# Moving a weight read behind a head's operands, cutting GpSimd's operations into 256-column pieces, and computing three kinds of small factors on ScalarE

## The chip, the cores and the metric

One core of a Trainium2 chip runs the whole program. The metric is the device time in microseconds (us) of one execution. The engines are TensorE (PE), which multiplies, VectorE (DVE), ScalarE (ACT) and GpSimd (POOL), which do the elementwise work, and SyncE (SP), which here issues the DMA transfers.

## The reference

The kernel computes a two-layer decoder trunk for 512 tokens of width 1024 in float32. Between two feed-forward halves each layer has a mixer of three groups of heads that run side by side on one input projection:

```python
for l in range(DEPTH):                                  # DEPTH = 2
    x = x + 0.5 * swiglu(rmsnorm(x, ffn1_norm[l]), ffn1_wg[l], ffn1_wu[l], ffn1_wd[l])
    h = rmsnorm(x, mix_norm[l]) @ w_in[l]
    h_a, h_b, h_c = jnp.split(h, [A_COLS, A_COLS + B_COLS], axis=-1)
    o_a = mla_mixer(h_a, ...)       # 6 heads, low-rank q and kv, rope on 32 of 96 columns
    o_b = nsa_mixer(h_b, ...)       # 6 heads: compressed, selected and window attention, gated
    o_c = diff_mixer(h_c, ...)      # 4 heads: softmax 1 - lam * softmax 2
    x = x + jnp.concatenate([o_a, o_b, o_c], axis=-1) @ w_out[l]
    x = x + 0.5 * swiglu(rmsnorm(x, ffn2_norm[l]), ffn2_wg[l], ffn2_wu[l], ffn2_wd[l])
return rmsnorm(x, final_norm)

# nsa_mixer: g = sigmoid(gate_logits); o = g0 * o_cmp + g1 * o_slc + g2 * o_win
#            compress: silu(blocks @ w1) @ w2
# diff_mixer: o = o1 - lam * o2, then a norm over each head's 64 columns
```

## The kernel before

Activations lie transposed in SBUF: 128 features on the partitions, 512 tokens in the free dimension. To keep float32 accuracy each operand of a matmul is split into a rounded high part and the rest (`split`: ACT copies or scales into `hi`, and DVE or POOL subtracts it for `lo`, L162 and L164, or L166 with a scale), and each product takes three passes (`mm3`, `mm3y`: hi*hi, hi*lo, lo*hi).

A layer goes ffn1, mix, ffn2. The feed-forward parts stream weights through `weights()`: a 512 KB read into `raw`, then a split into `whl`. While ffn1 runs, `split_ahead` does this for the eight column groups of `w_in` named in `AHEAD = (2, 0, 1, 3, 9, 8, 5, 4)` and parks the split pair of 1 MB in a DRAM buffer (`pre<-whl`). In the mix `weights()` finds the key in `PRE` and needs a read only (`whl<-pre`, L185).

The mix first projects the columns of the C heads (differential attention). Each result is split and written to two DRAM buffers by `put` (`part<-b`, L755), and `c_load(h)` reads one head's operands back in another layout: six reads `qk<-part` (L194) for head 0, then six for each further head. The period table `PLAN` then sets the order of PE's work in the rest of the mix: in each row the front (scores) of one head, the back (weighing the values) of the head before it, and `items` such as `p2 p0 cl1 cl2` (projections of column groups 2 and 0, loads of C heads 1 and 2) are interleaved step by step. A front (`scores`) computes score rows in PSUM; DVE takes the negated row maximum (`nmx`, L595), ACT the exponential with the row sum (`pn`, L596), DVE a reciprocal; `turned` transposes the probabilities on PE (`pst`, L573), and ACT and DVE split them into `pt`. In `c_front` the second softmax's factor is multiplied by -lam (L825), ACT scales the rows of the second softmax with it (L827), and DVE adds the rows of the first (L828). At L886 to L890 the NSA gate is made: exp on ACT, plus one on DVE (L889), reciprocal on DVE. L1020 to L1022 do the same for the silu of the compression.

PE's order within the mix is the program's. The order of the other engines and of SP's queue is set when the kernel is built, by a scheduler with a timeline of its own. POOL takes `split`s with `eng=gp` (the weight tiles 128x1024 and others, the query heads in `SPARE`), the products of the rotary embedding (`rope`, `roped`, `a_query`: L556, L557, L729, L730, L952, L953), the slow reciprocal root (`rsqrt_slow`: L211, L212, L214) and one sum of squares (L866).

## Time and profile before

| quantity | value |
|---|---|
| median of 3 runs | 2020.51 us (2019.13 to 2026.75) |
| the profiled execution | 2023.87 us |
| its span in the trace | 2022.1 us |
| PE busy | 1968.2 us (97%) |
| DVE busy | 1473.4 us (73%) |
| ACT busy | 1066.5 us (53%) |
| POOL busy | 253.5 us (13%) |
| DMA queue of SP | 286.48 MB, 45.5% of 16 engines' span |

Times inside the profile count from the start of the span. Busy shares are means over stages with different limits: in the two feed-forward parts PE has no gaps, and most of its idle time lies in the two mixes (about 380 to 660 us and 1380 to 1660 us) and at the two ends of the program. The profiled execution lies 3.36 us above the median of the three runs, and inside their range.

### The profile page before, as it was taken

To read this page: it belongs to the slowest core of one execution; us is meant where nothing else is said; L and a number is where in the kernel's file an instruction comes from. 1 tells how busy PE (TensorE), PEld (TensorE's weight loads), DVE (VectorE), ACT (ScalarE), POOL (GpSimd) and SP (SyncE) were. 2 spreads that over 40 slices of the span, in tenths; PEclk is the share of its full clock that TensorE was granted. 3 is DMA by queue.
4 is the path that set the end of the run, shared out by engine and by line. 5 is a ranking of instruction groups with operands and counts; after the bars stand their busy time and mean duration, and the time that the engine had idled before them with its cause. 6 is when DMAs were issued, how large, how long until landed. Compare 5 with 4: busy or idle time off the path is not lost.

```text
span 2022.1 us, 31129 instructions
## 1 busy us (share of the span) xinstructions
PE 1968.2 (97%) x11864; PEld 1711.7 (85%) x11864; DVE 1473.4 (73%) x2315; ACT 1066.5 (53%) x2010; POOL 253.5 (13%) x183
## 2 busy tenths in 40 slices
PE   8999999989999999999999999999989999999997
PEld 6899988867777899998889999887668778999886
DVE  8888874478887888883378887444898878888623
ACT  4455643266687545562255556333667764555521
POOL 5000001025420100001100000110354010000011
PEclk9999999999999999999999999999999999999999
DMA  6333388664632523334442335777447143333431
GB/s 209 105 105 105 114 282 266 207 213 129 179 105 81 170 94 105 105 118 138 131 143 88 106 107 170 245 230 228 158 135 214 53 146 115 95 106 106 133 114 55
DMA packets 104549, 288.46 MB, mean 143 GB/s; under 512 B 14928, under 2 KB 18768, under 8 KB 104400
## 3 DMA queue, kind: packets, MB, share of 16 engines
q1 hardware_dynamic: 104400, 286.48, 45.5%
q8 instruction: 93, 1.52, 0.3%
q14 instruction: 56, 0.46, 0.1%
HBM read 237.77 MB, written 46.66 MB: 141 GB/s over the span
## 4 chain that ended last, share of the span: by engine, by line
PE 83%; DVE 8%; DMA 2%; ACT 2%; issue 2%; SPq 1%; POOL 1%; DVEq 0%; ACTq 0%; POOLq 0%
PE psm L562 19%; PE psm L203 14%; PE pss L562 11%; PE pst L203 10%; PE pst L562 9%; PE pss L203 8%; PE pso L562 6%; PE pso L203 5%; PE pst L573 1%; DVE nmx L595 1%; DVE pt L164 1%; DMA part<-b 1%; DVE b L166 1%; DMA qk<-part 1%; SPq L194 1%
## 5 line engine op out<-in xcount | busy, mean ns | idle before, releaser
L162 ACT CAST whl<-raw 128x1024 fp32r<-128x1024 f32 (+2 forms) x417 | 383.8, 923 | 489.8 <-issue 104.8
L164 DVE TENSOR_TENSOR whl<-raw,whl 128x1024 fp32r<-128x1024 f32 (+2 forms) x383 | 420.1, 1099 | 222.2 <-ACT whl L162 221.4
L562 PE MATMUL psm<-b,whl 128*128 128x256 f32 (+1 forms) x2140 | 448.6, 346 | 3.6 <-DVE t L951 3.6
L562 PEld LDWEIGHTS psm<-b,whl 128*128 128x128 f32 x2140 | 328.8, 192 | 44.5 <-issue 8.0
L203 PE MATMUL psm<-b,whl 128*128 128x512 f32 (+1 forms) x948 | 230.6, 383 | 1.2 <-DVE whl L164 1.0
L298 POOL TENSOR_TENSOR t<-t,t 128x512 f32<-128x512 f32 x48 | 78.3, 1632 | 1104.2 <-ACT t L292 777.4
L203 PEld LDWEIGHTS psm<-b,whl 128*128 128x128 f32 x948 | 174.7, 189 | 36.5 <-DVE whl L164 1.4
L203 PE MATMUL pst<-b,whl 128*128 128x512 f32 x624 | 158.6, 394 | 3.0 <-DVE b L166 1.2
L203 PEld LDWEIGHTS pst<-b,whl 128*128 128x128 f32 x624 | 117.3, 189 | 31.3 <-DVE b L166 3.1
L596 ACT ACTIVATE pn<-pss,nmx 128x256 f32<-128x256 f32 x208 | 109.6, 528 | 64.6 <-DVE nmx L595 63.3
L595 DVE TENSOR_REDUCE nmx<-pss 128x1 f32<-128x256 f32 x208 | 97.7, 485 | 42.2 <-PE pss L562 30.9
L203 PE MATMUL pss<-b,whl 128*128 128x512 f32 x504 | 126.3, 390 | 0.0
L562 PE MATMUL psm<-qk,whl 128*128 128x256 f32 x840 | 123.7, 284 | 0.0
L562 PE MATMUL pst<-b,whl 128*128 128x256 f32 (+1 forms) x816 | 121.2, 290 | 0.2 <-DVE b L164 0.2
L562 PE MATMUL pss<-b,whl 128*128 128x256 f32 (+1 forms) x816 | 120.8, 290 | 0.0
L562 PEld LDWEIGHTS psm<-qk,whl 128*128 128x128 f32 x840 | 111.2, 192 | 0.3
L203 PEld LDWEIGHTS pss<-b,whl 128*128 128x128 f32 x504 | 94.7, 188 | 19.5
L562 PEld LDWEIGHTS pst<-b,whl 128*128 128x128 f32 x816 | 108.5, 192 | 2.9 <-DVE b L164 0.5
L562 PEld LDWEIGHTS pss<-b,whl 128*128 128x128 f32 x816 | 108.9, 192 | 2.1
L164 DVE TENSOR_TENSOR whl<-pn,whl 128x1024 fp32r<-128x1024 f32 x63 | 77.2, 1226 | 26.2 <-ACT whl L162 26.2
L562 PE MATMUL pst<-qk,whl 128*128 128x256 f32 x576 | 84.8, 284 | 0.0
L562 PE MATMUL pss<-qk,whl 128*128 128x256 f32 x576 | 84.8, 283 | 0.0
(314 smaller groups left out, 3402.6 us busy)
## 6 DMA issues: line engine op xcount, KB each, us to landing
raw<-in_ffn_gu_dram SPq DMA_DIRECT2D x174, 512.0 KB, 3.7
raw<-in_ffn_d_dram SPq DMA_DIRECT2D x64, 512.0 KB, 3.7
pre<-whl SPq DMA_DIRECT2D x16, 1024.0 KB, 5.5
whl<-pre SPq DMA_DIRECT2D x16, 1024.0 KB, 7.0
raw<-in_w_in_dram SPq DMA_DIRECT2D x28, 512.0 KB, 6.0
raw<-in_ffn_d_dram SPq DMA_DIRECT2D x32, 384.0 KB, 3.4
xin<-xs SPq DMA_DIRECT2D x48, 256.0 KB, 3.0
raw<-in_w_out_dram SPq DMA_DIRECT2D x32, 256.0 KB, 2.8
```

The lines of the kernel that those rows point to most:

```text
L162: high = sc.copy(hi, src) if scale is None else sc.mul(hi, src, scale)
L164: eng.tensor_tensor(lo, src, f32(hi), op=ALU.subtract)
L166: eng.scalar_tensor_tensor(lo, src, scale, f32(hi), op0=ALU.mult, op1=ALU.subtract)
L194: return sy.dma_start(f32(dst), f32(src))
L203: pe.matmul(ps, w(a), x(b), start=first and k == 0 and j == 0, stop=last and k == n - 1 and j == 2)
L298: gp.tensor_tensor(sq, sq, self.acc, op=ALU.add)
L562: return tc.keep_in_program_order(pe.matmul(*args, **kw))
L573: return tc.keep_in_program_order(pe.transpose(dst, src, idn))
L595: ve.reduce_max(nmx, part[i], axis=AX.X, negate=True)
L596: sc.activation(pn[i], part[i], AF.Exp, bias=nmx, accum_out=sm[:, i:i + 1])
```

## The change

It does three things. First, `c_load` keeps the last of head 0's six operand reads in `S["cl0"]`, and the read of a pre-split weight tile in `project` (`whl<-pre`) is put behind it in the order of issue, for every column group but the first of `AHEAD`. Secondly, a helper `pieces` issues a `tensor_tensor` of POOL with a 2-dimensional output as pieces of 256 columns; it is used by `split`, `rsqrt_slow`, `rope`, `roped`, `a_query` and the sum L866. Calls with DVE as the engine go through it unchanged, and POOL's other operations (L294, L296, L298, L326, L1078, L1079) don't use it. Thirdly, three kinds of small steps become ACT instructions: the factor times -lam, and the two "plus one" steps of the gate and of the silu, which add a constant tile `onet` as bias.

```diff
--- before.py
+++ after.py
@@ -157,11 +157,19 @@
     def f32(ap):
         return ap.bitcast(F32) if ap.dtype == F32R else ap
 
+    def pieces(eng, o, a, b, op):
+
+        n = o.shape[1]
+        m = P * 2 if eng is gp and len(o.shape) == 2 else n
+        for c in range(0, n, m):
+            d = min(c + m, n)
+            eng.tensor_tensor(o[:, c:d], a[:, c:d], b[:, c:d], op=op)
+
     def split(src, hi, lo, scale=None, eng=ve):
 
         high = sc.copy(hi, src) if scale is None else sc.mul(hi, src, scale)
         if scale is None:
-            eng.tensor_tensor(lo, src, f32(hi), op=ALU.subtract)
+            pieces(eng, lo, src, f32(hi), op=ALU.subtract)
         else:
             eng.scalar_tensor_tensor(lo, src, scale, f32(hi), op0=ALU.mult, op1=ALU.subtract)
         return high
@@ -178,11 +186,12 @@
         d = PRE[key] = dp.tile([P, 2, 8 * P], F32, name=nm("pre"))
         sy.dma_start(d, f32(hl[:, :, :8 * P]))
 
-    def weights(src, rows=P, cols=8 * P, eng=gp, key=None):
+    def weights(src, rows=P, cols=8 * P, eng=gp, key=None, behind=None):
 
         if key in PRE:
             hl = wp.tile([P, 2, WPAD], F32R, tag="whl", name=nm("whl"), bufs=WHLS)
-            sy.dma_start(f32(hl[:, :, :8 * P]), PRE.pop(key))
+            with tc.issue_after(behind.ins) if behind else ExitStack():
+                sy.dma_start(f32(hl[:, :, :8 * P]), PRE.pop(key))
             return hl
         raw, hl = weight_tiles()
         sy.dma_start(raw[:rows, :cols], src)
@@ -208,10 +217,10 @@
         sc.activation(y, ps, AF.Ln, bias=epst, scale=mul)
         sc.activation(ms, ps, AF.Identity, bias=epst, scale=mul)
         sc.activation(y, y, AF.Exp, scale=-0.5)
-        gp.tensor_tensor(r, y, y, op=ALU.mult)
-        gp.tensor_tensor(r, r, ms, op=ALU.mult)
+        pieces(gp, r, y, y, op=ALU.mult)
+        pieces(gp, r, r, ms, op=ALU.mult)
         sc.activation(r, r, AF.Identity, bias=halft, scale=-0.5)
-        gp.tensor_tensor(r, r, y, op=ALU.mult)
+        pieces(gp, r, r, y, op=ALU.mult)
         return r
 
     def rsqrt(ps, mul, r):
@@ -264,6 +273,8 @@
     gp.memset(epst, EPS)
     halft = cp.tile([P, 1], F32, name="halft")
     gp.memset(halft, 1.5)
+    onet = cp.tile([P, 1], F32, name="onet")
+    gp.memset(onet, 1.0)
 
 
     xs = [I["xT"]]
@@ -553,8 +564,8 @@
         t, sw = tmp()[r0:r1], tmp()[r0:r1]
         ve.stream_shuffle(sw, src, swap)
         ve.tensor_tensor(t, src, cos[r0:r1], op=ALU.mult)
-        eng.tensor_tensor(sw, sw, sin[r0:r1], op=ALU.mult)
-        eng.tensor_tensor(t, t, sw, op=ALU.add)
+        pieces(eng, sw, sw, sin[r0:r1], op=ALU.mult)
+        pieces(eng, t, t, sw, op=ALU.add)
         return t
 
     def mm(*args, **kw):
@@ -693,7 +704,8 @@
 
         def project(c, done, eng=gp):
 
-            w = weights(I["w_in"][l, c], eng=ve if "w%d" % c in SPARE else eng, key=("in", l, c))
+            w = weights(I["w_in"][l, c], eng=ve if "w%d" % c in SPARE else eng, key=("in", l, c),
+                        behind=S.get("cl0") if c != AHEAD[0] else None)
             pj = psum("m")
             yield from mm3y(pj, [((lambda a, k=k: w[:, a, k * P:(k + 1) * P]), (lambda b, k=k: xg[k][:, b])) for k in range(KD)])
             done(pj)
@@ -726,8 +738,8 @@
             c, sw = tmp()[:n], tmp()[:n]
             ve.stream_shuffle(sw, t[:n], swap)
             ve.tensor_tensor(c, t[:n], loaded(tabs[g, 0])[:n], op=ALU.mult)
-            eng.tensor_tensor(sw, sw, loaded(tabs[g, 1])[:n], op=ALU.mult)
-            eng.tensor_tensor(t[:n], c, sw, op=ALU.add)
+            pieces(eng, sw, sw, loaded(tabs[g, 1])[:n], op=ALU.mult)
+            pieces(eng, t[:n], c, sw, op=ALU.add)
             return t
 
         def scales(n):
@@ -811,7 +823,8 @@
                 src = S["C"][c].rearrange("j (d h m) n -> j d h (m n)", h=4, m=2)[:, :, h]
                 dst = qk[c].rearrange("p m n -> p (m n)")
                 for j in range(3):
-                    move(dst[32 * j:32 * j + 32], src[PASS[j][1 - c]])
+                    done = move(dst[32 * j:32 * j + 32], src[PASS[j][1 - c]])
+            S.setdefault("cl0", done)
 
         def c_front(h):
             qk = S["cqk", h]
@@ -822,7 +835,7 @@
                 ve.reciprocal(o[1], o[1])
                 pns.append(o)
             (p1, s1), (p2, s2) = pns
-            ve.tensor_scalar(s2, s2, S["nlam"], None, op0=ALU.mult)
+            sc.mul(s2, s2, S["nlam"])
             for j in range(NT):
                 sc.mul(p2[j], p2[j], s2[:, j:j + 1])
                 ve.scalar_tensor_tensor(p1[j], p1[j], s1[:, j:j + 1], p2[j], op0=ALU.mult, op1=ALU.add)
@@ -863,7 +876,7 @@
             t = S["at1"] = scaled(pj, rs[0])
             q = tmp()
             sc.activation(q[:64], t[:64], AF.Square)
-            gp.tensor_tensor(S["aq0"][:64], S["aq0"][:64], q[:64], op=ALU.add)
+            pieces(gp, S["aq0"][:64], S["aq0"][:64], q[:64], op=ALU.add)
             ca1 = S["ca1"] = halves(t[:64], mg[:64, 1:2])
 
             kp = rope(t[64:96], loaded(tabs[0, 0]), loaded(tabs[0, 1]), SWAP16, 64, 96)
@@ -886,7 +899,7 @@
             gate = S["gate"] = small([P, NT, 32], "gate", bufs=1)
             gf = gate.rearrange("p i c -> p (i c)")
             sc.activation(gf, gps[:, :P], AF.Exp, scale=-1.0)
-            ve.tensor_scalar(gf, gf, 1.0, None, op0=ALU.add)
+            sc.activation(gf, gf, AF.Identity, bias=onet)
             ve.reciprocal(gf, gf)
             yield
 
@@ -949,8 +962,8 @@
             t, sw = tmp(), tmp()
             ve.tensor_tensor(t[:96], pj[:96], ta[:96, 0], op=ALU.mult)
             ve.stream_shuffle(sw[64:96], pj[64:96], SWAP16)
-            gp.tensor_tensor(sw[64:96], sw[64:96], ta[64:96, 1], op=ALU.mult)
-            gp.tensor_tensor(t[64:96], t[64:96], sw[64:96], op=ALU.add)
+            pieces(gp, sw[64:96], sw[64:96], ta[64:96, 1], op=ALU.mult)
+            pieces(gp, t[64:96], t[64:96], sw[64:96], op=ALU.add)
             split(t[:96], q[:96, 0], q[:96, 1], eng=gp if "hq%d" % h in SPARE else ve)
 
         def a_front(h):
@@ -1018,7 +1031,7 @@
             ve.scalar_tensor_tensor(z[:, :, 0:31], p3[0:64, :, 0:31], bias, y1[:, :, 1:32], op0=ALU.add, op1=ALU.add)
             e = small([64, 2, 32], "ce", bufs=1)
             sc.activation(e, z, AF.Exp, scale=-1.0)
-            ve.tensor_scalar(e, e, 1.0, None, op0=ALU.add)
+            sc.activation(e, e, AF.Identity, bias=onet[:64])
             ve.reciprocal(e, e)
             ve.tensor_tensor(z, z, e, op=ALU.mult)
             zh = S["z", n] = small([64, 2, 64], "czh", F32R)
```

The number of PE's instructions and their order stay as they were. DVE has 14 instructions fewer, ACT 14 more, and POOL 117 more. All lines of the changed file lie further down (L185 becomes L194, L194 becomes L203, L755 becomes L767, L595 and L596 become L606 and L607, L162 and L164 become L170 and L166, which is `pieces`).

SP's queue at the start of layer 0's mix, ahead of the first C head; `whl` are weight tiles, `pre` the parked split weights, `part` the DRAM buffers of the C heads, `qk` the head operands. Before:

```order
L185 DMA whl_3845<-pre_2808 128x2x1024
L755 DMA part_3535<-b_3642 64x2x512
L755 DMA part_3536<-b_3642 64x2x512
L194 DMA qk_3647<-part_3535 32x1024 x3
L194 DMA qk_3648<-part_3536 32x1024 x3
L194 DMA qk_3914<-part_3535 32x1024 x3
L194 DMA qk_3915<-part_3536 32x1024 x3
L194 DMA qk_3922<-part_3535 32x1024 x3
L194 DMA qk_3923<-part_3536 32x1024 x3
L185 DMA whl_3957<-pre_2960 128x2x1024
L185 DMA whl_4043<-pre_3060 128x2x1024
```

And with the change:

```order
L767 DMA part_3537<-b_3644 64x2x512
L767 DMA part_3538<-b_3644 64x2x512
L203 DMA qk_3649<-part_3537 32x1024 x3
L203 DMA qk_3650<-part_3538 32x1024 x3
L194 DMA whl_3847<-pre_2810 128x2x1024
L203 DMA qk_3916<-part_3537 32x1024 x3
L203 DMA qk_3917<-part_3538 32x1024 x3
L203 DMA qk_3924<-part_3537 32x1024 x3
L203 DMA qk_3925<-part_3538 32x1024 x3
L194 DMA whl_3959<-pre_2962 128x2x1024
```

The weight read `whl_3845` (now `whl_3847`, column group 0) stood ahead of the last two writes of `part`; now it stands behind them and behind the first six `qk` reads, and twelve more `qk` reads follow it. Layer 1 moves in the same way.

DVE at the NSA gate in layer 0, between the row maxima of two heads; `gate` is the gate tile. Before:

```order
L728 TENSOR_TENSOR t_4101<-t_4099,xin_4104 128x512
L595 TENSOR_REDUCE nmx_4176<-pss_4172 128x1
L889 TENSOR_SCALAR gate_4153<-gate_4153 128x128
L890 RECIPROCAL gate_4153<-gate_4153 128x128
L595 TENSOR_REDUCE nmx_4179<-pss_4172 128x1
L595 TENSOR_REDUCE nmx_4185<-pss_4182 128x1
L595 TENSOR_REDUCE nmx_4205<-pss_4202 128x1
```

And with the change:

```order
L740 TENSOR_TENSOR t_4106<-t_4104,xin_4109 128x512
L606 TENSOR_REDUCE nmx_4186<-pss_4182 128x1
L903 RECIPROCAL gate_4163<-gate_4163 128x128
L606 TENSOR_REDUCE nmx_4189<-pss_4182 128x1
L606 TENSOR_REDUCE nmx_4195<-pss_4192 128x1
L606 TENSOR_REDUCE nmx_4215<-pss_4212 128x1
```

The sum L889 is gone from between the maximum and the reciprocal; ACT has it now as L902, ahead of the exponential of the same head.

DVE at the fourth C head in layer 0; `sm` are the head's factors, `pn` its probabilities, `t` and `b` the work of other heads. Before:

```order
L164 TENSOR_TENSOR peh_5063<-pe_5061,peh_5063 64x32
L822 RECIPROCAL sm_4407<-sm_4407 128x4
L720 TENSOR_TENSOR t_4512<-psm_4467,rstd_3499 128x512
L825 TENSOR_SCALAR sm_4407<-sm_4407,nlam_3545 128x4
L166 SCALAR_TENSOR_TENSOR b_4438<-t_4167,dn_3539,b_4438 128x512
L166 SCALAR_TENSOR_TENSOR b_4514<-t_4512,b_4514 128x512
L828 SCALAR_TENSOR_TENSOR pn_4331<-pn_4331,sm_4332,pn_4406 128x128
L828 SCALAR_TENSOR_TENSOR pn_4331<-pn_4331,sm_4332,pn_4406 128x256
L828 SCALAR_TENSOR_TENSOR pn_4331<-pn_4331,sm_4332,pn_4406 128x384
L828 SCALAR_TENSOR_TENSOR pn_4331<-pn_4331,sm_4332,pn_4406 128x512
L632 TENSOR_TENSOR t_4565<-pso_4524,t_4565 64x512
```

And with the change:

```order
L166 TENSOR_TENSOR peh_5104<-pe_5102,peh_5104 64x32
L835 RECIPROCAL sm_4420<-sm_4420 128x4
L732 TENSOR_TENSOR t_4531<-psm_4486,rstd_3501 128x512
L174 SCALAR_TENSOR_TENSOR b_4454<-t_4177,dn_3541,b_4454 128x512
L174 SCALAR_TENSOR_TENSOR b_4533<-t_4531,b_4533 128x512
L643 TENSOR_TENSOR t_4584<-pso_4543,t_4584 64x512
L841 SCALAR_TENSOR_TENSOR pn_4344<-pn_4344,sm_4345,pn_4419 128x128
L841 SCALAR_TENSOR_TENSOR pn_4344<-pn_4344,sm_4345,pn_4419 128x256
L841 SCALAR_TENSOR_TENSOR pn_4344<-pn_4344,sm_4345,pn_4419 128x384
L841 SCALAR_TENSOR_TENSOR pn_4344<-pn_4344,sm_4345,pn_4419 128x512
```

The factor L825 is gone from between the two products, and the sum L632 (now L643) stands ahead of the four row sums L828 (now L841) instead of behind them.

## Rows read from the trace of the kernel before

**Rows 1.** The page, busy time of each engine: PE.

```profile
PE 1968.2 (97%) x11864; PEld 1711.7 (85%) x11864; DVE 1473.4 (73%) x2315; ACT 1066.5 (53%) x2010; POOL 253.5 (13%) x183
```

**Rows 2.** PE's waits over the whole span: total us, times, longest.

```profile
PE pss L562 <- ACT pn L596: 9.8, 19, 1.8
...
PE pss L562 <- DMA qk<-part: 6.1, 2, 4.0
```

**Rows 3.** Timeline of PE: start, us, instructions; in brackets the wait before and its releaser.

```profile
401.54 0.42 PE L562 MATMUL pss<-qk,qk 96*128 96x256 f32 x2 [2.12 <-DMA qk<-part]
...
407.61 2.09 PE L562 MATMUL psm<-b,whl 128*128 128x512 f32 x8
...
439.27 0.50 PE L562 MATMUL pss<-qk,qk 96*128 96x512 f32 x1 [1.82 <-ACT pn L596]
...
482.40 0.41 PE L573 MATMUL pst<-cst,pn 128*128 128x128 f32 x2 [2.25 <-DVE pt L164]
...
1400.17 0.66 PE L562 MATMUL pss<-qk,qk 96*128 96x256 f32 x2 [3.97 <-DMA qk<-part]
```

**Rows 4.** Windows behind those waits: window us, PE busy, PEclk, DMA share, GB/s.

```profile
401.82:405.23 3.41, 3.41 (x12) 0.50 1.01 233
483.74:487.15 3.41, 3.41 (x15) 0.50 0.87 223
1398.52:1405.35 6.83, 5.18 (x15) 0.50 1.01 234
```

**Rows 5.** Timeline of SP's queue, 386 to 404: start, us to issue, transfers.

```profile
386.81 0.56 SPq L185 DMA_DIRECT2D whl<-pre  x1
387.46 2.15 SPq L755 DMA_DIRECT2D part<-b  x2
395.71 8.23 SPq L194 DMA_DIRECT2D qk<-part  x18
```

**Rows 6.** The chain that ended last, three of its pieces: start, us, what.

```profile
387.46 8.10 DMA part<-b
...
397.96 3.34 DMA qk<-part
...
1385.56 10.30 DMA part<-b
```

**Rows 7.** DMA to landing: first L755's six writes from 380.8, then all of L185.

```profile
DMA to landing us min/median/max: 4.9/5.9/6.1
...
DMA to landing us min/median/max: 5.2/7.0/10.8
```

**Rows 8.** Windows of 20 us: PE, PEld, DVE, ACT, POOL, PEclk, DMA share, GB/s.

```profile
400.00:420.00 20.00, 17.91 (x76) 13.16 (x77) 10.35 (x24) 11.61 (x32) 1.56 (x1) 0.91 1.01 286
...
500.00:520.00 20.00, 17.24 (x87) 12.61 (x88) 18.36 (x35) 11.04 (x27) 13.96 (x9) 0.95 0.48 139
```

**Rows 9.** DVE's groups by form, 395 to 560: busy us, mean ns, idle before.

```profile
L825 DVE TENSOR_SCALAR sm<-sm,nlam 128x4 f32<-128x4 f32 x4 | 2.5, 637 | 0.1
L889 DVE TENSOR_SCALAR gate<-gate 128x128 f32<-128x128 f32 x1 | 1.0, 985 | 0.0
```

**Rows 10.** Timelines of DVE and of POOL, 471 to 476.

```profile
472.10 1.87 DVE L825 TENSOR_SCALAR sm<-sm,nlam 128x4 f32<-128x4 f32 x1
473.88 1.85 DVE L166 SCALAR_TENSOR_TENSOR b<-t,dn,b 128x512 fp32r<-128x512 f32 x1
...
471.54 2.40 POOL L164 TENSOR_TENSOR whl<-raw,whl 128x1024 fp32r<-128x1024 f32 x1
473.89 1.29 POOL L164 TENSOR_TENSOR qk<-t,qk 96x512 fp32r<-96x512 f32 x1
```

**Rows 11.** POOL's groups by form, whole span: busy us, mean ns, idle before.

```profile
L164 POOL TENSOR_TENSOR whl<-raw,whl 128x1024 fp32r<-128x1024 f32 x10 | 24.8, 2478 | 6.7 <-ACT whl L162 6.2
...
L729 POOL TENSOR_TENSOR t<-t,xin 64x512 f32<-64x512 f32 x2 | 5.5, 2760 | 5.8 <-DVE t L727 5.8
L326 POOL TENSOR_TENSOR pn<-b,rstd 128x256 f32<-128x256 f32 x6 | 4.9, 849 | 15.1 <-DVE rstd L226 15.1
```

**Rows 12.** ACT's groups by form, 395 to 560: busy us, mean ns, idle before.

```profile
L888 ACT ACTIVATE gate<-pst 128x128 f32<-128x128 f32 x1 | 0.3, 278 | 0.0
```

## Prediction

> **What bounds the kernel now.** I read the busy line of the page first: TensorE (PE) works for 1968.2 of the 2022.1 us span [rows 1]. So nothing but PE's standstills and its slow stretches can be won, unless its matmuls change, and the change leaves all of them and their order alone. What is left is 53.9 us (2022.1 less 1968.2), and some of that is the start and the end of the program. Next I read PE's waits by releaser: 9.8 us for the exponentials of the score rows on ScalarE (ACT), and 6.1 us, in only two waits, for reads of `qk` tiles out of the DRAM buffer `part` [rows 2]. The timeline of PE then gives the places, and each of those this part speaks of recurs in layer 1, about 1000 us later: 2.12 and 3.97 us before the first C head's scores, 1.82 us at the NSA gate (1.81 in layer 1), and 2.25 us at the fourth C head (2.26 in layer 1) [rows 3]. [...]
>
> **Part 1: the read of the second pre-split weight tile goes behind the first head's operands.** The queue of SyncE (SP) issues six writes of `part`, then the 1 MB read `whl<-pre`, then the last two writes, and then the `qk` reads [rows 5]. The reads wait for the writes: the chain that ended last has 8.10 us in the writes behind the weight read, and then 3.34 us in the last `qk` read that the scores need [rows 6]. The first six writes, with no weight read straight ahead of them, landed 4.9 to 6.1 us after their issue [rows 7]. Without the read ahead, the pair starts at 386.81 in place of 387.46, and its last write, issued some 0.9 us later, lands by 387.7 + 4.9 to 6.1 = 392.6 to 393.8. SP's first `qk` issue in before was at 395.71 and the sixth read landed at 397.96 + 3.34 = 401.30, 5.6 us later; moved, that is 398.2 to 399.4. PE asks for it at 401.54 - 2.12 = 399.42: the wait goes. In layer 1 the writes took 10.30 us from 1385.56 [rows 6]; at 6.1 us, and 0.65 us earlier, they end at 1391.0 instead of 1395.9, 4.9 us sooner, and the 3.97 us wait goes as well. With the two half-clock stretches this removes 2.12 + 3.97 + 1.7 + 2.6 = 10.4 us.
>
> What is late next is the weight read itself. It now passes two writes and six `qk` issues and starts at 395 to 396 (sixth issue), while twelve more `qk` reads queue behind it, half a microsecond apart (8.23 us for 18 [rows 5]). Reads of this kind took 5.2 to 10.8 us, in the middle 7.0 [rows 7], and the DMA engines were full from 400 to 420 (share 1.01 [rows 8]). Issued at 395.8 it lands at 402.8, at worst at 406.6. Its first user is the matmul group at 407.61 [rows 3], which, with 2.12 + 1.7 us saved ahead of it, comes at 403.8. By the middle value the read is just hidden; by the worst PE waits 2.8 us, and some 1 us more in layer 1, where more time is saved ahead of the need. I charge 0.7 us per layer. **Part 1: 10.4 - 1.4 = 9.0 us gained**, at most 10.4, at least 3 (first rival).
>
> **Part 2: three kinds of small steps move from VectorE (DVE) to ACT.** For each layer these are four factors (128x4), one gate sum (128x128) and two 64x64 sums. On DVE they cost far more than their size: 637 ns mean for the 128x4, 985 for the 128x128 [rows 9]. The timeline shows why: the 128x4 step that began at 472.10 took 1.87 us and ended at 473.97, when GpSimd's (POOL) 1024-wide subtraction, begun at 471.54, ended at 473.94; the next DVE step, 1.85 us, ended after POOL's next one (473.89 to 475.18) [rows 10]. So a DVE instruction of this form stands behind the whole POOL instruction that is running. ACT does a 128x128 step in 278 ns [rows 12], and I take 0.25 us for each moved step, so 14 of them are 3.5 us on ACT over both layers, in places where it mostly waits for DVE. At the gate the DVE steps sum, reciprocal and the next row maximum stand in the way of the exponential that PE waits for. The sum's 0.98 us leaves that chain, since ACT has it ready while DVE still works on the maximum before it: 0.95 per layer, 1.9 in all. At the fourth C head 1.87 us leave DVE, ahead of the transposed rows that PE waits 2.25 us for: I take 1.8 per layer, 3.6 in all, and half of the one half-clock stretch there, 0.9. If ACT is full when its extra step comes, it costs up to its 0.25 us; this I expect at the first C head, 0.2 per layer.
>
> [...]
>
> **Part 3: POOL's 2-dimensional operations in the mix go in pieces of 256 columns**, 117 instructions more in both layers. A 1024-wide subtraction took 2478 ns, or 620 per 256 columns; the 256-wide operation that the kernel has took 849 [rows 11]. So a further piece costs at most 0.23 us, at least 0 if pieces overlap. I take 0.15 (nearer the upper end, since the 849 ns may hold waiting): 18 us of POOL time over two mixes, in which POOL has room. What it frees is DVE, which then waits for one piece of about 0.7 us and not for up to 2.48. Of PE's 9.8 us of waits for exponentials 1.82 + 1.81 were counted; of the 6.2 us left in 17 waits I take a third, 2.0 us, since here I can name no single piece that carries all. Against it 0.5 us for POOL results that come later. **Parts 2 and 3: 1.9 + 3.6 + 0.9 + 2.0 - 0.4 - 0.5 = 7.5 us gained**, between 0 (all of it turns into the next wait) and about 14 (most of the named waits and their clock).
>
> **Sum.** 9.0 + 7.5 = 16.5 us off. The profiled execution was 2023.87 us, 3.4 above the median of 2020.51, so it becomes 2007.4 and the median 2004.0.
>
> **The rivals.** (a) *The weight read takes the wait over.* For it: DMA is full there and 1 MB cannot land faster because it is put later. Against it: by the middle value it has 1 us to spare. At 10.8 us PE waits 2.8 us and 3.8 us in the two layers: with 1.4 already charged that takes 5.2 more, and a clock fall 1.4: 2010.6. (b) *DVE remains the bound in the middle.* DVE was busy 18.36 of 20 us in 500:520 [rows 8]; PE's waits there may only move along, so that 9.0 us of part 1 is all: 2011.5. That includes the case that pieces do not release DVE any earlier. (c) *The other side: POOL becomes the bound.* In 500:520 POOL was busy 13.96 us with nine instructions [rows 8]; these get some eleven more pieces, and POOL's idle 6.04 us allows 0.55 us for each. This decides it: at 0.15 to 0.23 there is room, but DVE blocks POOL too: the 64x512 product took 2760 ns [rows 11], 1.5 us over the half of 2478 that its 512 columns should take, or 0.75 for each of two DVE steps. If one such step gets in at each piece, a piece costs 0.23 + 0.75 = 0.98, POOL needs 13.96 + 10.8 = 24.7 us for 20, and with two such stretches in each layer it is 4 x 4.7 = 18.8 us late, with a half-clock stretch of 1.7 us behind each: 25.6 lost, parts 2 and 3 worth nothing, part 1 kept: 2020.5 + 25.6 - 9.0 = 2037. [...]
>
> **How the numbers follow.** Forecast (12 to 23 us gained) 0.57; rival (a) 0.12; rival (b) 0.18; rival (c) or a part of it 0.08; more than 23 us gained 0.05. The median is 2004; its own range is 1997 to 2009. For 8 in 10 I reach from 1996 (nearly the upper bounds of both sums, 10.4 + 14) to 2016 (part 1 at its least, 3 us, and 1.5 of the rest), leaving out (c) and the tails. Half a per cent, about what a measurement of this kernel can tell from no change, is 10.1 us, so the bound of faster is 2010.4. Faster: 0.55 of the forecast, 0.07 of (a), 0.04 of (b) and 0.05: 0.71. Same: 0.02, 0.05, 0.13 and 0.02 of (c): 0.22. Slower: 0.06, and 0.01 of (b): 0.07.
>
> **What would show it.** Part 1 is right if the waits for `qk<-part` at the first C head are gone and the clock stays at 1.00 there in both layers; it is wrong if PE waits there for `whl<-pre`. Part 2 is right if the gate's wait falls by about 0.95 us, and the fourth C head's to under 0.5. Part 3 is right if DVE's long steps (over 1.2 us at 512 columns) shrink while POOL's time per column grows by under 10%; wrong if new PE waits appear for chains that pass through POOL. The whole is wrong most likely by (b), where each wait gets shorter and the next one longer.

## The result and the profile after

The changed kernel took 2012.72 us (median of 5 runs, 2010.17 to 2014.30) against 2026.02 for the kernel before (5 runs). The ratio is 0.9941, with a 95% interval of 0.9923 to 0.9959, so about 12 us faster, with 8 to 16 inside the interval (the two medians lie 13.3 us apart). The forecast was 16.5 us, at the lower edge of whose band of 12 to 23 us this falls; its median of 2004.0 us started from the 2020.51 that the first three runs of the kernel before gave, and with two more runs that kernel stands at 2026.02. A second group of runs gave 0.9938 (0.9925 to 0.9950).

Names in the changed kernel: L194 is the read `whl<-pre`, L203 the `qk` reads, L606 and L607 the row maximum and the exponential, L170 ACT's half of a split, L166 the subtraction and every piece, L174 the split with a scale, L838 the factor times -lam, L841 the sum of the two softmaxes, L964 the rotary shuffle of a query head.

The page's busy line of the changed kernel, beside [rows 1]:

```profile
PE 1963.1 (98%) x11864; PEld 1708.8 (85%) x11864; DVE 1462.0 (73%) x2301; ACT 1069.8 (53%) x2024; POOL 281.7 (14%) x300
```

DVE has 11.4 us less, ACT 3.3 more, and POOL 28.2 more (forecast: 18). PE's waits over the whole span, as in [rows 2]:

```profile
PE pst L584 <- DVE pt L166: 9.8, 10, 3.0
PE pss L573 <- ACT pn L607: 6.8, 15, 0.9
PE psm L573 <- DVE t L964: 6.4, 2, 3.7
```

The 6.1 us for `qk<-part` are gone. The waits for exponentials fell from 9.8 to 6.8 us. But the waits of the query heads (`psm` behind L964) and of the transposed rows (`pst` behind DVE's `pt`) grew. Before they were:

```profile
PE pst L573 <- DVE pt L164: 8.3, 10, 2.3
...
PE psm L562 <- DVE t L951: 3.6, 2, 1.8
```

SP's queue, beside [rows 5]:

```profile
379.66 7.49 SPq L767 DMA_DIRECT2D part<-b  x8
390.49 2.89 SPq L203 DMA_DIRECT2D qk<-part  x6
393.42 0.57 SPq L194 DMA_DIRECT2D whl<-pre  x1
394.03 9.09 SPq L203 DMA_DIRECT2D qk<-part  x12
```

The `qk` reads start at 390.49 and no longer at 395.71. Next the timeline of PE at the gate, at the fourth C head and at the query head's projection, then the last two of these in layer 1 ([rows 3] has those of before):

```profile
433.06 0.50 PE L573 MATMUL pss<-qk,qk 96*128 96x512 f32 x1 [0.80 <-ACT pn L607]
...
475.16 0.66 PE L584 MATMUL pst<-cst,pn 128*128 128x128 f32 x2 [3.04 <-DVE pt L166]
...
511.39 2.58 PE L573 MATMUL psm<-b,whl 128*96 128x512 f32 x6 [2.72 <-DVE t L964]
...
1467.63 0.51 PE L584 MATMUL pst<-cst,pn 128*128 128x128 f32 x2 [3.05 <-DVE pt L166]
...
1502.73 2.69 PE L573 MATMUL psm<-b,whl 128*96 128x512 f32 x5 [3.73 <-DVE t L964]
```

The same places of the kernel before that its rows did not show (the query head of layer 0, then the fourth C head and the query head of layer 1):

```profile
516.50 2.05 PE L562 MATMUL psm<-b,whl 128*96 128x512 f32 x6 [1.79 <-DVE t L951]
...
1481.99 0.30 PE L573 MATMUL pst<-cst,pn 128*128 128x128 f32 x1 [2.26 <-DVE pt L164]
...
1513.77 2.47 PE L562 MATMUL psm<-b,whl 128*96 128x512 f32 x6 [1.79 <-DVE t L951]
```

PE's order is the same in both kernels, so the start of one matmul in both is a clock for the lead. At the gate of layer 0 the changed kernel leads by 439.27 - 433.06 = 6.21 us, at the fourth C head by 482.40 - 475.16 = 7.24, at the query head by 516.50 - 511.39 = 5.11. In layer 1 the last two are 14.36 and 11.04. So 2.1 us are given back between the fourth C head and the query head in layer 0, and 3.3 us in layer 1. The clock does its part, as windows of the changed kernel show (columns as in [rows 8]; the first two are the first C head in either layer, the last two the fourth):

```profile
396.00:406.00 10.00, 10.00 (x50) 7.84 (x49) 5.05 (x13) 5.41 (x17) 0.00 (x0) 1.00 0.92 269
1388.00:1398.00 10.00, 10.00 (x51) 7.82 (x49) 5.04 (x13) 5.38 (x17) 0.00 (x0) 1.00 0.98 284
...
474.53:481.36 6.83, 6.20 (x24) 5.21 (x25) 4.05 (x10) 3.42 (x10) 0.00 (x0) 0.50 0.73 192
...
1467.81:1471.22 3.41, 3.41 (x13) 2.49 (x12) 2.08 (x5) 1.73 (x6) 0.00 (x0) 0.50 0.87 267
```

At the first C head PE is never idle and its clock stays at 1.00 in both layers. At the fourth C head of layer 0 the stretch at half clock (granted 0.50) is now 6.83 us long, 6.20 of it busy, where it was 3.41 before [rows 4]. In layer 1 it is 3.41 us long, and before there was none there.

What holds the fourth C head? Timelines of DVE and of POOL of the changed kernel, 469 to 475:

```profile
470.75 3.00 DVE L174 SCALAR_TENSOR_TENSOR b<-t,b 128x512 fp32r<-128x512 f32 x1 [0.41 <-ACT b L170]
...
469.73 1.42 POOL L166 TENSOR_TENSOR qk<-t,qk 96x256 fp32r<-96x256 f32 x2
471.12 3.22 POOL L166 TENSOR_TENSOR whl<-raw,whl 128x256 fp32r<-128x256 f32 x4
```

DVE's step began at 470.75 and ended at 473.75. A step of its kind takes 0.69 us (the same line and shape at 465.39 of this kernel). It did not get in behind the piece that was running: with 0.69 us of its own it can have entered at 473.06 at the earliest, when the third of the four weight pieces was at its end (they start at 471.12, 471.80, 472.49 and 473.2, the first three take 0.72 to 0.73 us, the fourth 1.17). Behind it on DVE stood two row maxima and then the subtraction `pt` of rows that PE had transposed, which PE's next transposes waited for. And 36 us later, DVE's own 1024-wide weight subtraction, which stands ahead of L964, overlapped POOL's pieces of a rotary product:

```profile
507.00 1.75 DVE L166 TENSOR_TENSOR whl<-raw,whl 128x1024 fp32r<-128x1024 f32 x1
```

It took 1.21 us in the kernel before. The prices of the new steps, groups by form of the changed kernel over the whole span (POOL, then ACT):

```profile
L166 POOL TENSOR_TENSOR whl<-raw,whl 128x256 fp32r<-128x256 f32 x86 | 71.3, 853 | 177.2 <-ACT whl L170 173.1 <-issue 2.0 <-POOL t L166 1.7
...
L838 ACT ACTIVATE sm<-sm,nlam 128x4 f32<-128x4 f32 x8 | 2.3, 293 | 5.2 <-DVE sm L835 5.2
...
L902 ACT ACTIVATE gate<-gate,onet 128x128 f32<-128x128 f32 x2 | 0.8, 408 | 0.0
```

### The profile page after: what moved, and what is told of

Read it like the earlier page. It is cut to its first block, busy times and chain, and to the rows that moved or that the text cites. A ratio compares the mean times of both kernels' runs of the same rounds, so it can differ in the third digit from the quotient of the medians.

```text
span 2010.6 us, 31242 instructions
## 1 busy us (share of the span) xinstructions
PE 1963.1 (98%) x11864; PEld 1708.8 (85%) x11864; DVE 1462.0 (73%) x2301; ACT 1069.8 (53%) x2024; POOL 281.7 (14%) x300
## 4 chain that ended last, share of the span: by engine, by line
PE 88%; DVE 6%; ACT 2%; POOL 2%; DMA 1%; issue 1%; SPq 0%; DVEq 0%; ACTq 0%; POOLq 0%
PE psm L573 23%; PE psm L212 14%; PE pss L573 11%; PE pst L212 9%; PE pst L573 9%; PE pss L212 8%; PE pso L573 6%; PE pso L212 5%; PE pst L584 1%; DVE nmx L606 1%; DVE pt L166 1%; POOL t L309 1%; ACT pn L607 1%; DVE b L174 1%; DVE pn L651 0%
## 5 line engine op out<-in xcount | busy, mean ns | idle before, releaser
L170 ACT CAST whl<-raw 128x1024 fp32r<-128x1024 f32 (+2 forms) x417 | 383.9, 923 | 488.6 <-issue 102.4
L166 DVE TENSOR_TENSOR whl<-raw,whl 128x1024 fp32r<-128x1024 f32 (+2 forms) x383 | 420.7, 1101 | 222.6 <-ACT whl L170 221.8
L607 ACT ACTIVATE pn<-pss,nmx 128x256 f32<-128x256 f32 x208 | 109.7, 528 | 53.4 <-DVE nmx L606 52.5
L606 DVE TENSOR_REDUCE nmx<-pss 128x1 f32<-128x256 f32 x208 | 97.5, 485 | 37.1 <-PE pss L573 25.3
L166 POOL TENSOR_TENSOR whl<-raw,whl 128x256 fp32r<-128x256 f32 (+2 forms) x90 | 75.2, 860 | 177.2 <-ACT whl L170 173.1
L166 DVE TENSOR_TENSOR whl<-pn,whl 128x1024 fp32r<-128x1024 f32 x63 | 77.2, 1225 | 26.3 <-ACT whl L170 26.3
```

What stands on the lines that cost most here:

```text
L166: eng.tensor_tensor(o[:, c:d], a[:, c:d], b[:, c:d], op=op)
L170: high = sc.copy(hi, src) if scale is None else sc.mul(hi, src, scale)
L606: ve.reduce_max(nmx, part[i], axis=AX.X, negate=True)
L607: sc.activation(pn[i], part[i], AF.Exp, bias=nmx, accum_out=sm[:, i:i + 1])
```

## The experiments

The first question is which part made the gain, and why the sum of the parts isn't reached. All ratios are to the kernel before on the same chip, with 95% intervals; the kernel before ran at 2024 to 2025 us there, so 0.001 is 2.0 us.

| kernel | read | pieces | ScalarE steps | ratio | us |
|---|---|---|---|---|---|
| e1_read_only | yes | no | no | 0.9944 (0.9931 to 0.9958) | -11.3 |
| e2_pieces_only | no | yes | no | 0.9972 (0.9961 to 0.9984) | -5.7 |
| e3_act_only | no | no | yes | 0.9994 (0.9984 to 1.0003) | -1.2 |
| e4_read_and_act | yes | no | yes | 0.9931 (0.9918 to 0.9944) | -14.0 |
| e5_no_act | yes | yes | no | 0.9931 (0.9919 to 0.9944) | -14.0 |
| e6_no_read | no | yes | yes | 0.9990 (0.9978 to 1.0001) | -2.0 |
| c1_changed_again | yes | yes | yes | 0.9938 (0.9925 to 0.9950) | -12.6 |
| e7_w6_on_vector | yes | yes | yes | 0.9938 (0.9925 to 0.9950) | -12.6 |
| e8_no_pieces_w6 | yes | no | yes | 0.9928 (0.9913 to 0.9943) | -14.6 |
| e9_no_pieces_swap | yes | no | yes | 0.9946 (0.9931 to 0.9961) | -10.9 |
| e11_pieces_in_splits | yes | in splits | yes | 0.9929 (0.9915 to 0.9944) | -14.4 |

Each part is taken out of the changed kernel by one of three edits:

```diff
-                        behind=S.get("cl0") if c != AHEAD[0] else None)      # no read moved
+                        behind=None)
-        m = P * 2 if eng is gp and len(o.shape) == 2 else n                  # no pieces
+        m = n
-            sc.mul(s2, s2, S["nlam"])                # no steps on ScalarE: this one and the
+            ve.tensor_scalar(s2, s2, S["nlam"], None, op0=ALU.mult)   # two "plus one" steps alike
```

**e1_read_only** leaves the read alone.

> Only the weight read is moved; no pieces, no steps on ScalarE. Theory A (the two DMA waits and their half-clock stretches are worth 10.4 us, and nothing else of this kernel moves): 8 to 10.5 us faster than before, no wait of PE for qk<-part or whl<-pre, the gate's wait still 1.8 us and the fourth C head's still 2.2 to 2.3. Theory B (the changed kernel's gain came mostly from its small steps and pieces): under 5 us faster.

11.3 us faster: theory A, and a little above its range. The gate and the fourth C head were as expected (1.80 and 2.25 us). But in the profiled execution PE did wait for the weight read in layer 0, once for 2.09 us, and half clock followed (timeline and window of this kernel):

```profile
404.70 0.99 PE L573 MATMUL psm<-b,whl 128*128 128x512 f32 x2 [2.09 <-DMA whl<-pre]
...
404.93:408.34 3.41, 3.41 (x11) 2.73 (x11) 0.80 (x3) 1.02 (x4) 0.00 (x0) 0.50 0.74 208
```

That is rival (a) in one execution, the longest of the six timed (2012.61 to 2018.67 us). The changed kernel's first profile has no such wait, but e7_w6_on_vector has one of 1.49 us at the same place, and c1, e5, e8 and e9 have shorter ones, for this read or a later `whl<-pre` (0.37 to 1.19 us). So six of the nine profiles with the read moved have some wait for `whl<-pre`, 1.1 us per execution in the mean of the nine: the read's landing is close to its need.

**e2_pieces_only** leaves the pieces alone.

> Only GpSimd's pieces; the read and the small steps as before. Theory A (pieces do not free VectorE, they keep it waiting over several pieces, and cost GpSimd 10% or more): 2 to 8 us slower than before, PE's waits for t<-psm of the query heads above 1.8 us each, GpSimd busy about 28 us more. Theory B (a VectorE step waits for one piece of 0.7 us and no more): 2 to 5 us faster, VectorE's 128x4 factor at 0.5 us mean or less.

5.7 us faster: theory B, and my reading of the changed kernel's profile, theory A, is wrong as a general statement. The 128x4 factor, still on DVE here, fell to 278 ns from 637 [rows 9] (group by form); the gate's wait fell to 1.32 us (1.27 in layer 1), the fourth C head waited a little less than before, the query head more (timeline of PE):

```profile
L838 DVE TENSOR_SCALAR sm<-sm,nlam 128x4 f32<-128x4 f32 x8 | 2.2, 278 | 0.1
...
481.06 0.41 PE L584 MATMUL pst<-cst,pn 128*128 128x128 f32 x2 [2.04 <-DVE pt L166]
...
514.52 3.12 PE L573 MATMUL psm<-b,whl 128*96 128x512 f32 x6 [2.95 <-DVE t L964]
```

**e3_act_only** leaves the steps on ScalarE alone.

> Only the three kinds of small steps on ScalarE. Theory A (they take 0.6 to 1.9 us each off VectorE in front of waits of PE): 3 to 6 us faster, the gate's wait down from 1.8 to about 0.8 us in both layers, the fourth C head's from 2.25 to under 1. Theory B (ScalarE's longer queue gives it back, and the fourth C head's longer wait in the changed kernel is its doing): within 2 us of before, the fourth C head's wait at 2.5 us or more.

1.2 us, not to be told from nothing: theory B by the time. The gate's wait did fall, to 0.79 us. At the fourth C head the matmul that waited 2.25 us before doesn't wait any more, but 14 matmuls ahead of it PE now waits 2.31 us for one of the sums L841. Timelines of DVE and POOL, and PE's wait, at that head:

```profile
467.74 2.91 DVE L174 SCALAR_TENSOR_TENSOR b<-t,dn,b 128x512 fp32r<-128x512 f32 x1
470.58 1.77 DVE L174 SCALAR_TENSOR_TENSOR b<-t,b 128x512 fp32r<-128x512 f32 x1
...
472.88 4.04 DVE L841 SCALAR_TENSOR_TENSOR pn<-pn,sm,pn 128x128 f32<-128x128 f32 x4
...
467.18 2.92 POOL L166 TENSOR_TENSOR whl<-raw,whl 128x1024 fp32r<-128x1024 f32 x1
...
476.31 0.47 PE L584 MATMUL pst<-cst,pn 128*128 128x128 f32 x1 [2.31 <-DVE pn L841]
```

The reader is to see who stands behind POOL now: with the factor gone, the next step with two operands in SBUF took its place (2.91 us, with POOL's 1024-wide instruction from 467.18 to 470.10), then the next one (1.77), and later one of the four L841 steps (4.04 us for four, 1.93 before). The wait was not removed with the step that stood in it; it was passed on. ScalarE's longer queue, theory B's reason, is not what held PE.

**e4_read_and_act** is the change without the pieces.

> The change without the pieces. Theory A (pieces cost): 13 to 16 us faster than before, so 2 to 5 us faster than the changed kernel; the waits for t<-psm of the query heads back at about 1.8 us each. Theory B (pieces help, the small steps do not): 6 to 10 us faster than before, slower than the changed kernel.

14.0 us faster, and the query heads' waits are back at 1.78 us in both layers (timeline of PE, fourth C head and query head of layer 0):

```profile
476.65 0.41 PE L584 MATMUL pst<-cst,pn 128*128 128x128 f32 x2 [2.26 <-DVE pt L166]
...
508.97 2.63 PE L573 MATMUL psm<-b,whl 128*96 128x512 f32 x6 [1.78 <-DVE t L964]
```

That is theory A's range, but the interval reaches over the changed kernel's ratio, so whether the pieces cost or bring something on top of the other two is not shown by the time. The timelines show where they do either: the changed kernel is 1.49 us ahead of e4 at the fourth C head of layer 0 (475.16), and 2.42 us behind it at the query head (511.39); in layer 1 it is 1.65 us ahead and then 0.36 behind.

**c1_changed_again, e5_no_act and e6_no_read** complete the eight combinations.

> The changed kernel itself, beside the others of this group. Every theory: 10 to 14 us faster than before, as measured (0.9941 of before).

> The change without the small steps on ScalarE: the read and the pieces. The read alone gave 11.3 us, the pieces alone 5.7, read and small steps 14.0. Theory A (the gains do not add, because the same stretch of VectorE work bounds PE once any one of them is there): 11 to 14 us faster than before, at the level of the changed kernel. Theory B (the gains add, and the small steps spoil them in the changed kernel): 16 to 18 us faster, clearly ahead of the changed kernel.

> The change without the moved read: pieces and small steps. Theory A (not additive): 0 to 4 us faster than before, less than the pieces alone, with a fourth C head's wait of about 3 us and query heads' waits of 2.7 and 3.7 us as in the changed kernel. Theory B (the pieces keep their 5.7 us, and the changed kernel loses on the read): 5 to 8 us faster.

c1 gave 12.6 us, as expected. The 14.0 us of e5 are theory A's, though its interval (11.3 to 16.4) just reaches theory B's range; the 2.0 us of e6 (-0.2 to 4.5) are theory A's, and theory B's 5 to 8 are outside. So the gains do not all add: the three parts alone make 18.2 us and together 12.6, with an uncertainty of about 5 us on the difference. Read and pieces, 14.0 for a sum of 17.0, are within the noise of adding. Pieces without ScalarE steps give 14.0 us with the read, with them 12.6 (not told apart); pieces and ScalarE steps together give 2.0 where the pieces alone gave 5.7 (these two intervals share only 0.9978 to 0.9984). PE's waits at the fourth C head say where (timelines of e5_no_act and then of e6_no_read):

```profile
474.06 0.41 PE L584 MATMUL pst<-cst,pn 128*128 128x128 f32 x2 [2.05 <-DVE pt L166]
```

```profile
481.84 0.41 PE L584 MATMUL pst<-cst,pn 128*128 128x128 f32 x2 [3.05 <-DVE pt L166]
```

A wait of 3 us or more there stands only in kernels with both: pieces on POOL and the steps on ScalarE. In e2_pieces_only no DVE step up to the query heads takes over 1.76 us. Why it needs both is not shown. The same L174 step falls among the same four pieces in e5 too, but begins just before the fourth, and gets in at once (timelines of DVE and POOL of e5_no_act):

```profile
471.96 0.69 DVE L174 SCALAR_TENSOR_TENSOR b<-t,b 128x512 fp32r<-128x512 f32 x1 [0.37 <-ACT b L170]
...
469.92 3.32 POOL L166 TENSOR_TENSOR whl<-raw,whl 128x256 fp32r<-128x256 f32 x4 [0.40 <-ACT whl L170]
```

**e7_w6_on_vector** takes those four pieces away, in the changed kernel. Column group 6 of `w_in` is subtracted by DVE:

```diff
-SPARE = (..., 'hq3', 'w0', 'w2', 'w3', 'w7')
+SPARE = (..., 'hq3', 'w0', 'w2', 'w3', 'w6', 'w7')
```

> The changed kernel with one weight tile of each layer (column group 6 of w_in, 128x1024) subtracted by VectorE and not by GpSimd in four pieces. Theory A (VectorE's 3.00 us step before the fourth C head's transposes stood behind three back-to-back pieces of this tile): that step falls to about 0.7 us and the 1024-wide one of 1.2 us takes its place, so the wait of PE there falls from 3.0 to about 2 us in both layers, and the kernel gains 1 to 3 us on the changed one. Theory B (the step is late for another reason): the wait stays at 3 us or grows by the 1.2 us that VectorE now does itself.

The wait fell from 3.04 to 1.96 us in layer 0 and to 1.97 in layer 1, as theory A said (timeline of PE), and DVE's step from 3.00 to 1.22 us. The time doesn't show it: 0.9938, as the changed kernel in the same group, with 2.5 us of interval on either side of both, so a gain of 1 to 3 us is neither shown nor excluded.

```profile
476.24 0.41 PE L584 MATMUL pst<-cst,pn 128*128 128x128 f32 x2 [1.96 <-DVE pt L166]
...
509.70 2.96 PE L573 MATMUL psm<-b,whl 128*96 128x512 f32 x6 [2.84 <-DVE t L964]
```

**e8_no_pieces_w6** is e4 with the same exchange, **e9_no_pieces_swap** gives column group 7 to POOL in return (`'w6'` in place of `'w7'`).

> The read and the small steps, no pieces, and column group 6 of w_in subtracted by VectorE. Theory A (each remaining wait of PE ends with a VectorE step that stands behind GpSimd): the fourth C head's wait falls from 2.3 us to under 1.5, the query heads' waits stay at 1.8, and the kernel is 15 to 18 us faster than before, ahead of the changed kernel by 2 to 5. Theory B (VectorE's own load bounds the stretch, whoever holds it): 13 to 14.5 us faster, as the read and the small steps alone, with the saved time given back at the query heads.

> As the kernel before it in this group, but column group 7 goes from VectorE to GpSimd in exchange, so the 1.2 us step ahead of the query head's t<-psm leaves VectorE. Theory A (that step is what PE waits for there): the waits for t<-psm fall from 1.8 to under 1.2 us, 15 to 19 us faster than before. Theory B (GpSimd's whole 2.4 us instruction holds VectorE instead): the waits stay at 1.8 us or grow, 13 us faster or less.

e8 gave 14.6 us (11.5 to 17.6), between the two ranges, so the time doesn't decide; its fourth C head's wait fell in layer 1, to 1.37 us, and hardly in layer 0 (2.12). e9 gave 10.9, theory B: the fourth C head fell to 1.07, and the query head's wait grew to 2.67 us (timeline of PE of e9). Theory B's reason, POOL's whole instruction in the way there, fits that; no timeline of POOL or DVE of e9 shows it.

```profile
478.75 0.66 PE L584 MATMUL pst<-cst,pn 128*128 128x128 f32 x2 [1.07 <-DVE pt L166]
...
513.47 3.12 PE L573 MATMUL psm<-b,whl 128*96 128x512 f32 x6 [2.67 <-DVE t L964]
```

**e11_pieces_in_splits** keeps pieces in `split` alone; the other calls of `pieces` are `tensor_tensor` again:

```diff
-            pieces(eng, sw, sw, loaded(tabs[g, 1])[:n], op=ALU.mult)
+            eng.tensor_tensor(sw, sw, loaded(tabs[g, 1])[:n], op=ALU.mult)
...
```

> The changed kernel with pieces in the splits only; GpSimd's rotary products, the slow root and the sum of squares stay whole. Theory A (a rotary product in pieces lets GpSimd in between two VectorE steps at the query heads, and VectorE's 1024-wide step takes 1.76 us in place of 1.21): the waits for t<-psm are back near 1.8 to 2.2 us with the fourth C head's still at 3.0, 12 to 14 us faster than before. Theory B (PE only comes earlier there, and the wait ends when it ended): they stay at 2.7 to 3.7 us, 11.5 to 12.5 us faster.

Theory A by the query heads' waits, 1.78 and 2.33 us. The fourth C head's grew further, to 3.87 and 3.83, and the reason stands in the timelines of PE, DVE and POOL (the last line is PE at the query head):

```profile
475.66 0.66 PE L584 MATMUL pst<-cst,pn 128*128 128x128 f32 x2 [3.87 <-DVE pt L166]
...
470.43 3.83 DVE L174 SCALAR_TENSOR_TENSOR b<-t,b 128x512 fp32r<-128x512 f32 x1 [0.41 <-ACT b L170]
...
470.24 1.42 POOL L166 TENSOR_TENSOR qk<-t,qk 96x256 fp32r<-96x256 f32 x2
471.62 3.21 POOL L166 TENSOR_TENSOR whl<-raw,whl 128x256 fp32r<-128x256 f32 x4
...
509.65 3.12 PE L573 MATMUL psm<-b,whl 128*96 128x512 f32 x6 [1.78 <-DVE t L964]
```

The DVE step began just after the first of six pieces; at 0.69 us of its own it entered at 473.57, when five of them had run. At 14.4 us the kernel is still not told from the changed one.

**m1_ports**, a small kernel of its own that ran once, measures the contention by itself: POOL's subtractions of 128x1024 (L127), whole or in four pieces, and DVE's 128x512 steps with two operands in SBUF (L131), kept in written order.

> Not the trunk: a kernel of GpSimd subtractions 128x1024, whole or in four pieces, alone and against VectorE's 128x512 steps with two inputs in SBUF, first one behind the other, then with two or three steps out of PSUM between them. Theory A (VectorE gets in behind one piece): a VectorE step takes at most 0.7 + 0.7 = 1.4 us against pieces and up to 2.4 + 0.7 = 3.1 against whole instructions; four pieces cost 0.3 to 0.6 us more than the whole. Theory B (pieces that follow each other without a gap can keep VectorE out over several of them): some VectorE steps take over 2 us against pieces too.

All L131 or L127 instructions in stretches of this kernel (ns min/median/max): DVE alone; DVE against whole instructions; against pieces; against pieces with two PSUM steps between; then POOL alone, whole and in pieces:

```profile
L131 DVE SCALAR_TENSOR_TENSOR vt<-va,vb x8: 691/693/693, 3.5 to 8.6; 128x512 f32<-128x512 f32 x8
...
L131 DVE SCALAR_TENSOR_TENSOR vt<-va,vb x9: 691/2711/2806, 31.5 to 53.6; 128x512 f32<-128x512 f32 x9
...
L131 DVE SCALAR_TENSOR_TENSOR vt<-va,vb x16: 1094/1095/1190, 60.0 to 77.0; 128x512 f32<-128x512 f32 x16
...
L131 DVE SCALAR_TENSOR_TENSOR vt<-va,vb x8: 1215/1252/1253, 112.6 to 130.0; 128x512 f32<-128x512 f32 x8
...
9.92 9.66 POOL L127 TENSOR_TENSOR gt<-ga,gb 128x1024 f32<-128x1024 f32 x4
...
20.01 11.13 POOL L127 TENSOR_TENSOR gt<-ga,gb 128x256 f32<-128x256 f32 x16
```

Here theory A holds (the shortest step of the second row ran after POOL was done): against whole instructions a DVE step takes up to 2.81 us, against pieces never over 1.25, and 16 pieces take 11.13 us for 9.66, 0.37 us more for each 1024 columns. No step let more than one piece pass. So the steps of 3.00 and 3.83 us in the trunk are not what pieces do in this kernel.

## Why the prediction was right, and where its sum was off

**Part 1** was right in mechanism, and its size (9.0 us) was somewhat low: 11.3 us alone, with 8.5 to 14.0 inside the interval, and 10.5 us between e6_no_read and c1_changed_again (0.9990 to 0.9938). Both waits for `qk<-part` and the half clock behind them are gone (granted clock 1.00 at the first C head in both layers). The 1.7 and 2.6 us in its sum are half of PE's busy time in the two stretches at half clock [rows 4], an estimate: no run shows what the clock alone is worth there, only the 11.3 us for waits and clock together. What I named as late next, the weight read, cost 1.1 us of waits in the mean of nine profiles, where 1.4 were charged; rival (a) is real, but small. One reading was off: the first user of the read is not the matmul at 407.61 but one five matmuls ahead of it, where PE waits in e1 and e7, so the need came some 0.7 us earlier than reckoned.

**Part 2, the gate**, came out as worked out: the wait fell from 1.82 to 0.80 us, 1.02 for a forecast 0.95. The price on ScalarE was too low: 293 ns for the 128x4 factor and 408 for the gate in place of 250; it hurt nothing that the runs show.

**Part 2, the fourth C head** is the step that failed: "At the fourth C head 1.87 us leave DVE, ahead of the transposed rows that PE waits 2.25 us for: I take 1.8 per layer, 3.6 in all". The prediction had itself read the 1.87 us as a wait for POOL; what it left out is that POOL's instruction stays when the factor goes. e3 shows the next DVE step of two SBUF operands taking that wait over (2.91 us), and PE's wait of 2.25 us turning into one of 2.31 us for a later DVE step; with the pieces it was 3.04, where the sign asked for under 0.5. Of 3.6 + 0.9 us nothing shows in the time.

**Part 3** was mis-sized in both directions. The price of a further piece was 28.2 us over 117, 0.24 each, blocking by DVE included, just above the bound of 0.23 and not the 0.15 taken. Its signs failed: a piece of a weight tile took 853 ns where the whole instruction took 620 per 256 columns, over a third more and not under 10%, and DVE's long step grew to 3.00 us. Alone the pieces bring 5.7 us, more than the 2.0 counted net of 0.5. On top of the rest they bring nothing that the runs can tell: the changed kernel stands at 0.9938 and 0.9941, without pieces at 0.9931.

Parts 2 and 3 together were to bring 7.5 us and brought 1.2 (0.9944 to 0.9938, from two groups of runs, with 3.7 us of uncertainty on either side). So the whole came out at the lower edge of the forecast by part 1; that its surplus covered some of what the others lacked was luck.

In the time this is the outcome of rival (b), where parts 2 and 3 bring nothing. Its mechanism, waits of PE that only move along because DVE is the bound, fits the fourth C head in e3, but not the query head. There PE waits 1.78 or 1.79 us in before, e1, e3, e4 and e8, in both layers, though in e8 it gets there up to 12.5 us earlier than in before. The wait is 2.7 to 3.7 us in every kernel that cuts the rotary products into pieces, and 1.78 and 2.33 in e11, which leaves them whole. So of what the changed kernel gives back between the fourth C head and the query head, the longer waiting, 0.9 us in layer 0 and 1.9 in layer 1, is a price of part 3. The rest is about the half clock behind the fourth C head, by an estimate from the windows (half of the busy time in it, as a 128x512 matmul takes 0.50 us in e1's half-clock window and 0.26 at 407.61 of before, at a granted clock of 1.00) 1.4 us more than before in layer 0 and 1.7 in layer 1. That makes 2.3 and 3.6 us, for 2.1 and 3.3 of lead lost. These are single executions, and beside the read and the small steps the times with and without pieces are not told apart. Rival (c) did not come in its own form, POOL late for its users: no wait of PE in the mixes is put down to POOL. But that DVE and POOL hold each other up, its reason, is what the pieces cost there (DVE's 1024-wide step takes 1.75 us beside them, 1.21 before).

What stays open: why DVE's step let three pieces pass, and five in e11, in the trunk, where it lets one pass in m1_ports. Both came out of a short idle time behind an ACT release (0.41 us), into pieces that followed each other without a gap; so did the step of e5 (0.37 us), which got in at once. No run varied the moment of its start alone.

No version was shown to beat the changed kernel. e8 (0.9928) and e11 (0.9929) have the lowest ratios, inside its interval.

## What to carry to other kernels

A DVE step that looks expensive for its size may only be the one that stands in front of the door: before moving it, look at what POOL runs at that moment, and ask which step stands there next (here the 128x4 factor took 1.87 us beside POOL's 2.40, and once it was gone the step behind it took 2.91 beside POOL's 2.92). Parts of a change that each free the same engine ahead of the same chain should be summed as one, up to the wait that the chain leaves, and not one by one. A read that is needed late belongs behind reads that are needed early when they share a queue and busy DMA engines (here a share of 1.01 in the windows behind the late `qk` reads [rows 4], and 11.3 us gained in e1_read_only); the time of its own need, less what the change saves ahead of it, is the new limit.

## What the runs showed of the hardware

In m1_ports a DVE step with two SBUF operands waits for the POOL instruction that runs (2.71 us in the median for a 0.69 us step), while copies out of PSUM do not (686 ns in the mean of 56, beside whole POOL instructions and pieces); pieces of 256 columns bring the step to 1.10 us, for 15% more POOL time alone. The grain there is an instruction: no step took over 2.81 us beside whole ones of 2.67, and none over 1.25 beside pieces. The price of a piece is real (0.72 us for 256 columns, 2.34 for 1024, each with POOL alone), but e2_pieces_only was faster by 5.7 us. The waiting goes both ways: a POOL piece that takes 0.72 us alone took 1.17 in m1_ports when DVE steps alternated with it. And waits of one length need not cost the same: at the fourth C head of the kernel before, PE ran 3.41 us at half clock behind the 2.25 us wait of layer 0 and none behind the 2.26 us of layer 1; in the changed kernel it was 6.83 us at the 3.04 us wait and 3.41 at the 3.05.
